# One VectorE add moved ahead of two others in the first pair of six passes

## The chip, the cores and the metric

The kernel runs on one core of one Trainium2 chip. The time is the device time of one execution in microseconds (us); a smaller number is better. Every run named here is with a granted TensorE clock of 0.999 to 1.0.

## The reference

```python
h = x @ w1                         # x: 8 x 1024 x 1024, w1: 1024 x 4096
h = 0.5 * h * (1 + np.tanh(np.sqrt(2 / np.pi) * (h + 0.044715 * h ** 3)))
return (h @ w2).astype(np.float32) # w2: 4096 x 1024
```

Two matrix products with a gelu between them, for 8192 rows.

## The kernel before

The rows are worked in eight blocks of 1024. Each block has a pass called m1 (x @ w1 and the gelu) and a pass called m2 (times w2). Both use a scheme of seven products in place of eight block products; from the third block on (`sb > 1`), products 2 and 3 of m1 are once more split in this way, into seven parts each. An m1 goes through 16 column chunks in eight pairs `j`, with `h` the half of a pair. PSUM banks collect the products, ScalarE (ACT) copies a bank into a float32 buffer, and VectorE (DVE) adds later sums to it. `steps(m, ...)` is a generator that issues one split product in three stages:

```python
part(1, chain, True)                     # PE, into the left half of bank z
part(2, banks[0][:, left], fresh)
yield add(acc[0][:, left], chain)        # DVE reads the chain     (t0L for product 3)
part(6, chain)                           # PE writes the chain again
part(3, banks[0][:, right])
yield add(acc[0][:, right], chain)       # (t0R for product 3)
part(7, chain)
part(5, c5, fresh)
part(4, banks[1][:, left])
add(acc[1][:, left], chain)
... # two more adds for product 2, three for product 3
```

The body of a pair, with cuts:

```python
two = steps(2, source, cs, banks_b, a)
for h in range(2):
    ...                                  # in a first pair: a stage of two, five(h)
for _ in two:
    pass
for h in range(2):
    add(a[h], banks_b[h])                # DVE, 512 columns each
difference(j - 1)
...
def six(h):
    product(banks_a[h], source, 6, cs[h], False)
    act_copy(t[h], banks_a[h])
three = steps(3, source, cs, banks_c, t)
...                                      # not the last pair:
    first = j == 0
    five(0)
    if not first:
        gelu("11", cs[0], a[0])
    five(1)
    six(0)
    if not first:
        gelu("11", cs[1], a[1])
    if 3 in inner:
        next(three)                      # parts 1 and 2, t0L
        six(1)
        for h in range(2 if first else 0):
            gelu("11", cs[h], a[h])
        next(three)                      # parts 6 and 3, t0R
        seven(0)
        next(three)                      # part 7 and the rest
        seven(1)
```

In a first pair (`j == 0`) product 5 is already done inside product 2, so nothing but the adds stands between product 2 and `six(0)`. The helper `tt` in line 119 issues every add of VectorE; line 438 issues every matmul of m1, line 902 those of most m2 passes.

Of the kernel before, what the change touches and what calls it, by code (L numbers as in the profile page):

```python
# [61 lines left out]
def kernel(  # L62
# [46 lines left out]
    def psum():  # L109
        return pp.tile([P, HT], F32, name="ps")  # L110
# [23 lines left out]
    def act_copy(out, in_):  # L134
        tc.keep_in_program_order(nc.scalar.copy(out=out, in_=in_))  # L135
# [296 lines left out]
    def matmul1(xs, sb, quads, start=None):  # L432
        g = {b: gp.tile([P, NI, HT], GT, name=f"g{b}") for b in ("11", "12", "21", "22")}
        inner = INNER_1 if sb > 1 else ()
        left, right = slice(0, HT // 2), slice(HT // 2, HT)

        def multiply(bank, w, x, k, n, first):
            tc.keep_in_program_order(nc.tensor.matmul(  # L438
                bank, lhsT=w, rhs=x, start=first and k == 0, stop=k == n - 1, skip_group_check=not first,
            ))  # L440

        def product(bank, source, m, c, first):
            ops = source.chunk(m, c)
            for k in range(KH):
                multiply(bank, ops[:, k, :], xs[m][:, k, :], k, KH, first)

        def add(out, in1, in0=None):
            tt(out, out if in0 is None else in0, in1, ADD, True)
# [5 lines left out]
        def steps(m, source, cs, banks, acc):  # L454


            fresh = m == 2
            if m not in inner:
                yield product(banks[0], source, m, cs[0], fresh)
                yield  # L460
                yield product(banks[1], source, m, cs[1], fresh)
                return
            z = psum()
            c5 = banks[1][:, right] if fresh else z[:, right]
            chain = z[:, left]

            def part(j, out, first=False):
                for k in range(2):
                    if j in S_TERM:
                        h, b = (int(d) - 1 for d in S_TERM[j])  # L470
                        w = source.ops[m][:, 2 * b + k, h * P:(h + 1) * P]
                    else:
                        w = source.sums[m][:, list(S_SUM).index(j), k, :]
                    if j in W_TERM:
                        b, t = (int(d) - 1 for d in W_TERM[j])
                        x = xs[m][:, 2 * b + k, t * HT // 2:(t + 1) * HT // 2]
                    else:
                        x = xs.inner[m][:, SUMS.index(j), k, :]
                    multiply(out, w, x, k, 2, first)

            part(1, chain, True)
            part(2, banks[0][:, left], fresh)
            yield add(acc[0][:, left], chain)
            part(6, chain)
            part(3, banks[0][:, right])
            yield add(acc[0][:, right], chain)
# [4 lines that stand above are left out]
            add(acc[1][:, right], chain)  # L491
            add(acc[0][:, right], c5)
            if not fresh:
                add(acc[1][:, right], c5)
            yield
# [46 lines left out]
        for j in range(NI // 2):  # L542
            cs = (2 * j, 2 * j + 1)
            end = j == NI // 2 - 1
            if sb > 1:
                quads += [StoredHalf(i) for i in range(len(quads), min(j + 3, NI // 2))]
                source = quads[j]
            else:
                source = quads[j // 2]
            if start is not None and j == 0:  # L550
                start.pair(gelu)
                ahead(j)
                continue
            jobs = list(ahead(j))
            banks_a = [psum(), psum()]
            a = [temp(), temp()]
            for h in range(2):
                product(banks_a[h], source, 1, cs[h], True)
                act_copy(a[h], banks_a[h])
            banks_c, p5, t = [], [], [temp(), temp()]  # L560

            def five(h):
                if len(p5) == h:
                    banks_c.append(psum())
                    p5.append(temp())
                    product(banks_c[h], source, 5, cs[h], True)
                    act_copy(p5[h], banks_c[h])

            banks_b = [psum(), psum()]
            two = steps(2, source, cs, banks_b, a)  # L570
            more = xs.inner_jobs(3) if j == 0 and sb > 1 and 3 not in xs.inner else []
            for h in range(2):
                if late is not None:
                    gelu("12", late[1][h], late[3][h])
                if j == 0 or 2 in inner:
                    next(two)
                if late is not None:
                    product(late[2][h], late[0], 4, late[1][h], False)
                    gelu("21", late[1][h], late[2][h])
                elif j == 0:  # L580
                    for job in more[2 * h:2 * h + 2]:
                        job()
                    five(h)
            for _ in two:
                pass
            for h in range(2):
                add(a[h], banks_b[h])
            difference(j - 1)
            half = (len(jobs) + 1) // 2
            if start is not None and j == 1:  # L590
                rest = jobs[2:]
                half, jobs = 2, [lambda m=m: quads[0].sum(m, (2, 2), True) for m in (7, 4)] + jobs[:2]
            elif start is not None and j == 2:
                half, jobs = 2, rest
            if sb == 1:
                half = 3 if j % 2 else 0
                if j != 4:
                    jobs += splits
                    splits = []
            for job in jobs[:half]:  # L600
                job()
            def six(h):
                product(banks_a[h], source, 6, cs[h], False)
                act_copy(t[h], banks_a[h])

            def seven(h):
                product(banks_a[h], source, 7, cs[h], False)
                add(p5[h], banks_a[h])

            three = steps(3, source, cs, banks_c, t)  # L610
            if end:
                six(0)
                gelu("11", cs[0], a[0])
# [3 lines that stand above are left out]
                    five(h)  # L617
                for h in range(2):
                    seven(h)
                    gelu("22", cs[h], p5[h])  # L620
                    next(three)
                for h in range(2):
                    product(banks_a[h], source, 4, cs[h], False)
                    gelu("21", cs[h], banks_a[h])
                    for _ in three:
                        pass
                for h in range(2):
                    add(t[h], banks_c[h])
                    gelu("12", cs[h], t[h])
            else:  # L630
# [6 lines that stand above are left out]
                if not first:  # L637
                    gelu("11", cs[1], a[1])
                if 3 in inner:
                    next(three)  # L640
                    six(1)
                    for h in range(2 if first else 0):
                        gelu("11", cs[h], a[h])
                    next(three)
                    seven(0)
                    next(three)
                    seven(1)
                else:
# [3 lines that stand above are left out]
                    for _ in three:  # L652
# [3 lines that stand above are left out]
                for _ in three:  # L656
                    pass
                for h in range(2):
                    gelu("22", cs[h], p5[h])
                for h in range(2):  # L660
                    add(t[h], banks_c[h])
                late = (source, cs, banks_a, t)
            for job in jobs[half:]:
                job()
            if sb == 1 and j < 2 * len(SPLIT_IN_M1):
                splits = split_in_m1(SPLIT_IN_M1[j // 2], j % 2)
            steady(j)
# [361 lines left out]
    first = First()  # L1029
# [39 lines left out]
```

## Time and profile before

| | before |
|---|---|
| time, first three runs | 1487.91 us (1487.71 to 1488.25) |
| span of the profiled run | 1486.0 us |
| PE busy | 99% |
| VectorE busy | 77% |
| PE's waits for VectorE's adds, as shown | 2.3 us, 7 stops |

PE is the bound. What it loses to other engines is small, and of what the views show nearly all sits in six places. The prediction shows the lines. Two things help to read them. A group or a timeline row with a count merges several instructions. And the end of a matmul in the trace is modelled (one of 512 columns is shown 0.379 us long where starts are 0.216 us apart, one of 256 columns 0.272 us where they are 0.109 us apart), so the idle time shown before a matmul can be shorter than the delay of its start. I therefore count a **loss** from start to start: the distance of two matmuls' starts less the usual distance, 0.216 us after 512 columns and 0.109 us after 256. Counted like this, the six places lost 3.09 us; the six passes also have one stop of 0.325 us at 637 us, and 41 of 0.043 to 0.047 us, 1.9 us together, that no view lists.

### The profile page before, as it was taken

To read this page: it belongs to the slowest core of one execution; us is meant where nothing else is said; L and a number is where in the kernel's file an instruction comes from. 1 tells how busy PE (TensorE), PEld (TensorE's weight loads), DVE (VectorE), ACT (ScalarE), POOL (GpSimd) and SP (SyncE) were. 2 spreads that over 40 slices of the span, in tenths; PEclk is the share of its full clock that TensorE was granted. 3 is DMA by queue.
4 is the path that set the end of the run, shared out by engine and by line. 5 is a ranking of instruction groups with operands and counts; after the bars stand their busy time and mean duration, and the time that the engine had idled before them with its cause. 6 is when DMAs were issued, how large, how long until landed. Compare 5 with 4: busy or idle time off the path is not lost.

```text
span 1486.0 us, 26324 instructions
## 1 busy us (share of the span) xinstructions
PE 1477.3 (99%) x9879; PEld 964.2 (65%) x9879; DVE 1149.5 (77%) x1792; ACT 613.3 (41%) x1154; POOL 231.8 (16%) x311
## 2 busy tenths in 40 slices
PE   9999999999999999999999999999999999999998
PEld 5444444444455787558875588655886568855687
DVE  6657458767677898779987799877997779877887
ACT  5665026621166412663136621366214652056510
POOL 2542222222211012100022001210111101101011
PEclk9999999999999999999999999999999999999999
DMA  9999798987997999989999899998999989997886
GB/s 331 340 355 404 202 363 291 405 269 228 383 288 173 358 306 308 336 203 386 303 307 340 222 364 307 311 305 244 353 305 321 307 263 340 294 373 240 297 279 212
DMA packets 242719, 453.70 MB, mean 305 GB/s; under 512 B 80672, under 2 KB 85792, under 8 KB 241696
## 3 DMA queue, kind: packets, MB, share of 16 engines
q1 hardware_dynamic: 215680, 358.69, 71.6%
q0 software_dynamic: 26912, 93.34, 21.3%
q8 instruction: 77, 1.26, 0.3%
q14 instruction: 50, 0.41, 0.1%
HBM read 355.47 MB, written 111.15 MB: 314 GB/s over the span
## 4 chain that ended last, share of the span: by engine, by line
PE 97%; DVE 1%; DMA 1%; issue 0%; ACT 0%; DVEq 0%
PE ps L438 49%; PE ps L902 35%; PE ps L943 13%; PE ps L368 1%; DVE tmp L119 1%; DMA out_dram<-tmp 0%; PE ps L345 0%; DMA u<-in_x_dram 0%; DVE u L119 0%; ACT u L135 0%; ACT tmp L135 0%; PE ps L303 0%; DVE tmp L337 0%; DVE u L356 0%; DVEq L119 0%
## 5 line engine op out<-in xcount | busy, mean ns | idle before, releaser
L438 PE MATMUL ps<-u 128*128 128x512 f16 (+1 forms) x4104 | 746.7, 344 | 2.3 <-DVE tmp L119 2.3
L119 DVE TENSOR_TENSOR tmp<-tmp,ps 128x256 f32<-128x256 f32 (+1 forms) x930 | 450.7, 532 | 273.9 <-PE ps L438 169.4
L438 PEld LDWEIGHTS <-u 128*128 128x128 f16 x4104 | 401.1, 98 | 345.3 <-issue 11.0
L135 ACT COPY tmp<-ps 128x512 f32<-128x512 f32 x410 | 231.3, 581 | 302.1 <-PE ps L438 154.1
L451 ACT ACTIVATE g<-tmp 128x512 f16<-128x512 f32 x378 | 238.1, 633 | 165.2 <-DVE tmp L119 165.0
L902 PE MATMUL ps<-u,gc 128*128 128x256 f16 x2688 | 300.4, 273 | 0.0
L902 PEld LDWEIGHTS <-gc 128*128 128x128 f16 x2688 | 262.5, 98 | 31.2
L902 PE MATMUL ps<-u,g 128*128 128x256 f16 x2016 | 227.9, 273 | 0.0
L119 DVE TENSOR_TENSOR u<-u 128x2048 f16<-128x2048 f16 (+3 forms) x292 | 219.5, 790 | 9.2 <-DMA raw_d<-u 2.5
L135 ACT COPY u<-ps 128x512 f32<-128x512 f32 (+1 forms) x134 | 77.9, 587 | 348.9 <-PE ps L902 341.4
L902 PEld LDWEIGHTS <-g 128*128 128x128 f16 x2016 | 197.3, 98 | 24.1
L689 POOL DMA_DIRECT2D out_dram<-u x70 | 64.0, 989 | 710.5 <-issue 366.0
L119 DVE TENSOR_TENSOR u<-u,ps 128x512 f32<-128x512 f32 x216 | 147.7, 684 | 34.7 <-PE ps L902 28.5
L943 PE MATMUL ps<-u,g 128*128 128x512 f16 x768 | 166.4, 379 | 0.0
L943 PEld LDWEIGHTS <-g 128*128 128x128 f16 x768 | 75.1, 98 | 90.6
L119 DVE TENSOR_TENSOR g<-g,g 128x2048 f16<-128x2048 f16 (+1 forms) x136 | 130.3, 980 | 1.6 <-ACT g L451 1.6
L119 DVE TENSOR_TENSOR gc<-g,gc 128x2048 f16<-128x2048 f16 x84 | 102.4, 1219 | 0.6
L119 DVE TENSOR_TENSOR gc<-g 128x2048 f16<-128x2048 f16 x78 | 95.0, 1218 | 0.0
L451 ACT ACTIVATE g<-ps 128x512 f16<-128x512 f32 x134 | 79.9, 597 | 13.9 <-PE ps L438 6.9
L138 POOL CAST u<-gc 128x1024 f16<-128x1024 f32 x40 | 47.2, 1190 | 64.7 <-DMA gc<-in_w_dram 61.7
L415 POOL COPY pace<-g 128x2 f16<-128x2 f16 x24 | 4.4, 185 | 191.4 <-ACT g L451 191.4
L536 POOL TENSOR_TENSOR gc<-g 128x2048 f16<-128x2048 f16 x6 | 24.4, 4063 | 62.1 <-ACT g L451 62.1
(37 smaller groups left out, 257.3 us busy)
## 6 DMA issues: line engine op xcount, KB each, us to landing
u<-w_d SPq DMA_DIRECT2D x336, 256.0 KB, 6.5
u<-in_d SPq DMA_DIRECT2D x168, 512.0 KB, 7.1
u<-raw_d SPq DMA_DIRECT2D x252, 256.0 KB, 7.1
out_dram<-u POOLq DMA_DIRECT2D x70, 512.0 KB, 9.3
gc<-in_w_dram SPq DMA_DIRECT2D x48, 512.0 KB, 6.3
u<-in_d SPq DMA_DIRECT2D x96, 256.0 KB, 7.4
raw_d<-u SPq DMA_DIRECT2D x32, 512.0 KB, 8.9
u<-raw_d SPq DMA_DIRECT2D x32, 512.0 KB, 14.1
```

Of the source, the lines that this page charges most:

```text
L119: i = nc.vector.tensor_tensor(out=out, in0=in0, in1=in1, op=op)
L135: tc.keep_in_program_order(nc.scalar.copy(out=out, in_=in_))
L138: pool_last[0] = nc.gpsimd.tensor_copy(out=out, in_=in_)
L368: tc.keep_in_program_order(nc.tensor.matmul(bank[:, cols], lhsT=w[:, k, :], rhs=self.xs.blocks[f"{a}{r}"][:, k, cols], start=r == 1 and k ...
L415: mark = nc.gpsimd.tensor_copy(out=pace, in_=g_chunk[:, :2])
L438: tc.keep_in_program_order(nc.tensor.matmul(bank, lhsT=w, rhs=x, start=first and k == 0, stop=k == n - 1, skip_group_check=not first,))
L451: gelu_last[0] = nc.scalar.activation(out=g[b][:, c, :], in_=src, func=GELU)
L536: nc.gpsimd.tensor_tensor(out=early[7], in0=u, in1=v, op=SUB)
L689: return nc.gpsimd.dma_start(out=rows, in_=src, **kw)
L902: tc.keep_in_program_order(nc.tensor.matmul(bank[:, i * OH // 2:(i + 1) * OH // 2], lhsT=t[:, c, i * P:(i + 1) * P], rhs=self.y[j][:, c, : ...
L943: tc.keep_in_program_order(nc.tensor.matmul(pair(bank), lhsT=a[:, c, :], rhs=chunks(pieces[c // QC])[:, :, c % QC, :], start=(first and c ...
```

## The change

The intent: in the first pair of each of the six later m1 passes, let the first chain sum of product 3 (t0L) run before the two sums that end product 2, so that PE need not wait for it.

```diff
@@ -566,8 +566,21 @@
+            sixes = []
+
+            def six(h):
+                if h not in sixes:
+                    sixes.append(h)
+                    product(banks_a[h], source, 6, cs[h], False)
+                    act_copy(t[h], banks_a[h])
...          # seven and three are defined here too
             for _ in two:
                 pass
+            if j == 0 and 3 in inner:
+                six(0)
+                next(three)
             for h in range(2):
                 add(a[h], banks_b[h])
             difference(j - 1)
...
                 if 3 in inner:
-                    next(three)
+                    if not first:
+                        next(three)
                     six(1)
```

More of the change, by code (lines that the diff above doesn't have):

```diff
@@ L567, in five, with seven @@
                     act_copy(p5[h], banks_c[h])
+            sixes = []
[4 more added lines that the diff above has]
+                    act_copy(t[h], banks_a[h])
+            def seven(h):
+                product(banks_a[h], source, 7, cs[h], False)
+                add(p5[h], banks_a[h])
             banks_b = [psum(), psum()]
             two = steps(2, source, cs, banks_b, a)
+            three = steps(3, source, cs, banks_c, t)
             more = xs.inner_jobs(3) if j == 0 and sb > 1 and 3 not in xs.inner else []
@@ L601, in matmul1 @@
                 job()
-            def six(h):
-                product(banks_a[h], source, 6, cs[h], False)
-                act_copy(t[h], banks_a[h])
-            def seven(h):
-                product(banks_a[h], source, 7, cs[h], False)
-                add(p5[h], banks_a[h])
-            three = steps(3, source, cs, banks_c, t)
             if end:
```

## The prediction

The 1.73 us: from durations and pitches of the trace of the kernel before. In that trace an add of a bank took 0.67 to 0.69 us for 512 columns and 0.41 to 0.42 us for 256. That VectorE takes its adds in the order of its queue is read from the same trace: t0L's input was ready at 768.99 us, but t0L started at 769.49, behind the two sums. So is part 6's wait for t0L: t0L ended at 769.908 and part 6 started at 769.962. The eight banks that one rival counts are the pool of the program (`bufs=8`).

> **What bounds the kernel now.** I read the page first, then the PE's waits, then the chain of waits, then the timeline of one first pair instruction by instruction. The page's first part and its groups (engine, op, tiles, shape, count | busy us, mean ns | idle before, releaser):
>
> ```profile
> PE 1477.3 (99%) x9879; PEld 964.2 (65%) x9879; DVE 1149.5 (77%) x1792; ACT 613.3 (41%) x1154; POOL 231.8 (16%) x311
> ...
> L438 PE MATMUL ps<-u 128*128 128x512 f16 (+1 forms) x4104 | 746.7, 344 | 2.3 <-DVE tmp L119 2.3
> ```
>
> PE is busy for 1477.3 of 1486.0 us at full clock, so this change, which removes no matmul, can only win idle PE time. All idle time of the multiplication line that has a releaser is 2.3 us, and the releaser is the add helper of VectorE. The waits of PE give the same as a count:
>
> ```profile
> PE ps L438 <- DVE tmp L119: 2.3, 7, 0.6
> PE ps L303 <- DVE warm L1027: 1.2, 1, 1.2
> ```
>
> Seven waits. The whole chain of waits, in order of time, places them: it leaves PE for a run of VectorE adds ending at 409.5, 589.7, 769.9, 949.8, 1129.7 and 1309.7 us, which are the first pairs (j = 0) of the six later m1 passes, and once at 637.0, in a later pair. The piece of it for one first pair (start, us, what):
>
> ```profile
> 762.52 4.56 PE ps L438 x26
> ...
> 767.17 0.10 DVE tmp L119
> 767.27 0.24 issue
> 767.51 0.76 DVE tmp L119 x2
> 768.29 0.35 DVE tmp L119
> 768.65 0.25 issue
> 768.90 1.02 DVE tmp L119 x2
> 769.96 86.83 PE ps L438 x502
> ```
>
> After it PE runs 86.83 us without a break, so a microsecond won here comes off the end. Now the timeline of that pair, engine by engine. In program order VectorE ends product 2 with three 256-column adds of the chain and of the fifth term, then adds banks_b[0] and banks_b[1] (512 columns each), then the first chain sum of product 3, here called t0L:
>
> ```profile
> 767.17 1.08 DVE L119 TENSOR_TENSOR tmp<-tmp,ps 128x256 f32<-128x256 f32 x3 [0.28 <-PE ps L438]
> 768.29 1.28 DVE L119 TENSOR_TENSOR tmp<-tmp,ps 128x512 f32<-128x512 f32 x2
> 769.49 0.41 DVE L119 TENSOR_TENSOR tmp<-tmp,ps 128x256 f32<-128x256 f32 x1
> 770.38 0.42 DVE L119 TENSOR_TENSOR tmp<-tmp,ps 128x256 f32<-128x256 f32 x1 [0.47 <-PE ps L438]
> ```
>
> The third line is t0L, the fourth the second chain sum of product 3 (t0R). ScalarE copies product 6 (first line: t[0]), which t0L needs, and PE's part 6 of product 3 must wait until t0L has read the chain's bank:
>
> ```profile
> 768.40 0.59 ACT L135 COPY tmp<-ps 128x512 f32<-128x512 f32 x1 [0.93 <-PE ps L438]
> 769.70 0.59 ACT L135 COPY tmp<-ps 128x512 f32<-128x512 f32 x1 [0.71 <-PE ps L438]
> ```
>
> ```profile
> 769.96 0.60 PE L438 MATMUL ps<-u 128*128 128x256 f16 x4 [0.30 <-DVE tmp L119]
> ```
>
> t0L's input was ready at 768.99 (the copy's end), but it started at 769.49 because the two 512-column adds stood ahead of it. That is the fault that the change goes after.
>
> The shown 0.30 us of idle time is too small. Single matmuls of 512 columns start 0.216 us apart but are shown as 0.379 us long; so 0.163 us of every stop after one is hidden under its modelled end. From start to start, PE lost 0.459 us here: the last product-6 matmul started at 769.287, the next was due at 769.503 and came at 769.962. Counted like this over the trace, the six first pairs lost 0.446, 0.809, 0.459, 0.459, 0.456 and 0.460 us, together **3.09 us**. The 0.809 is the pair at 589.8: there VectorE's first add of the run began 0.35 us later after PE than in the others, for a reason that the trace does not give.
>
> [...]
>
> **The change part by part.** It adds and removes no instruction. For ScalarE and PE the order stays the same too: in a first pair product 5 has already been done inside product 2, so product 6 of half 0 was already PE's next work. What moves is one VectorE instruction: t0L goes ahead of the adds of banks_b[0] and banks_b[1]. It happens once in each of six m1 passes (inner product 3 exists only there).
>
> I work it out from s, the start of the last matmul of product 6, half 0 (767.987 in the pair above), with durations and pitches of that pair.
> 1. PE would be ready for part 6 at 0.216 + 4 x 0.109 (parts 1 and 2) + 4 x 0.216 (product 6, half 1) = s + 1.516.
> 2. The copy of t[0] starts at s + 0.416 and takes 0.586. An add that waits for ScalarE starts 0.033 later (the steady pairs: copies that end 33 ns before t0L starts), so t0L starts at s + 1.035; VectorE has been free since s + 0.27. t0L takes 0.42, and PE follows an add's end by 0.054: s + 1.51. So the wait at part 6 disappears. The steady pairs, which have this order already, lose 0.046 us there, with a busier ScalarE.
> 3. Part 6 and part 3 (4 x 0.109) and product 7, half 0 (4 x 0.216) follow; PE is then due for part 7, on the same chain, at s + 1.516 + 0.436 + 0.864 = s + 2.816. Part 7 must wait for t0R to read the chain.
> 4. VectorE's queue is now t0L, banks_b[0], banks_b[1], t0R. Start-to-start times: 0.338 after a 256-column add out of idle, 0.605 between 512-column adds, 0.597 from one of them to the next: t0R starts at s + 1.035 + 0.338 + 0.605 + 0.597 = s + 2.575, ends 0.414 later, and part 7 can start at s + 3.043.
> 5. So a **new wait of 0.227 us** stands at part 7, where there was none: before, t0R came right after part 6 and ended 0.46 us ahead of part 7's start (770.80 against 771.26).
> 6. After that VectorE is no worse off than before: the add of product 7 starts about s + 2.91 where it started at s + 3.47, and the rest follows PE.
>
> Net per pair: 0.446 - 0.227 = 0.22, four times about 0.458 - 0.227 = 0.23 (0.93 together), and 0.809 - 0.227 = 0.58 in the pair with the late add (its t0L waits for a copy ending at 588.46, and VectorE is free at 588.08, so the lateness is absorbed). Sum 0.22 + 0.93 + 0.58 = **1.73 us**. The loss of 3.09 us falls to 1.36 us. 1487.91 - 1.73 = 1486.2 us, 0.12% less.
>
> The two gelus of block 11 need the adds that now come later: banks_b[1] is summed at s + 1.978 + 0.68 = s + 2.66, and its gelu started at s + 2.73 before (770.715). It moves by little, and ScalarE is at 41%.
>
> **The rivals.** *All of it comes back* (1484.8 us): part 7 would not wait. For it: the change was presumably meant so. Against it: t0R stands behind two adds of 0.6 us each, and the sum of step 4 has only measured pitches in it. Part 7's dependence on t0R is in the code (same chain tile), hidden today by 0.46 us of slack.
>
> *The wait only moves* (1487.9 to 1489 us): t0L, now at the head of a FIFO and waiting for ScalarE, leaves VectorE idle from about s + 0.27 to s + 1.035, some 0.76 us that it used for the two sums. If a further hold of a few tenths comes in behind t0L, like the unexplained 0.35 us at 587, the new wait equals the old one. For it: the new wait is already half the old. Against it: VectorE has no other work queued in this stretch.
>
> *Another bank* (1489 to 1492 us): product 3's chain bank is now requested before the sums of product 2 are issued. If it got a bank that waits for one of them, PE would stop at part 1. Against it: of eight banks six are in use, product 2's chain is done and one is free; before, part 1 started (768.20) ahead of the sum of banks_b[0] (768.29), so it did not use that bank.
>
> **Range and chances.** The middle case takes 1.73 us, the full one 3.1, the moved one 0 or less. The three runs before span 1487.71 to 1488.25, a spread of 0.5 us. That gives 1485.3 to 1487.5 us. A change of 2% would be 30 us; only some 3.1 us of waits are touched, so nearly all the chance is on "same".
>
> **What would show it.** Right: in each first pair t0L starts some 0.46 us earlier after product 6, the wait before part 6 is gone, and a stop of about 0.23 us, shown as only 0.06 idle, stands before the first matmul of part 7; the PE's waits for VectorE fall from 2.3 to about 0.5 us shown; the span falls by about 1.7 us; the number of matmuls stays. The prediction is wrong if part 7 doesn't wait (then near 1484.8), if part 6 still waits, or if PE stops at part 1 of product 3 or at the first product of the next pair.

## The result, and the profile after

The changed kernel takes 1486.09 us (median of six, 1485.82 to 1486.73) against 1488.15 us (six runs, 1487.71 to 1488.64) of the kernel before. The ratio is 0.9987, with a 95% interval of 0.9974 to 1.0. Ratios here are the mean time of one kernel's fast runs over that of the other's of the same rounds, so not quite the ratio of the medians. A second set of five runs gave 1486.13 us and 0.9986 (0.9973 to 0.9998). Measured against 2% it is the same; the 1486.2 us foretold is 0.1 us off.

The page after, the line of engines and the group of m1's matmuls:

```profile
PE 1476.1 (99%) x9879; PEld 962.5 (65%) x9879; DVE 1146.3 (77%) x1792; ACT 613.5 (41%) x1154; POOL 225.3 (15%) x311
...
L438 PE MATMUL ps<-u 128*128 128x512 f16 (+1 forms) x4104 | 746.6, 344 | 0.5 <-DMA u<-w_d 0.2
```

The number of matmuls is unchanged, and the idle time in front of them fell from 2.3 to 0.5 us. PE's waits after (engine and line, what it waited for: us in total, times, longest):

```profile
PE ps L345 <- DVE tmp L337: 2.2, 4, 0.9
PE ps L303 <- DVE warm L1035: 1.2, 1, 1.2
PE ps L368 <- ACT u L135: 0.5, 1, 0.5
PE ps L368 <- DVE u L196: 0.4, 1, 0.4
PE ps L438 <- DMA u<-w_d: 0.2, 1, 0.2
```

The row in which line 438 waits for line 119 is gone; the 0.2 us for a transfer is the stop at 637 us, which was there before, under another releaser. Taken alone this view would say that all is won.

The spans of the two profiled runs, 1486.0 and 1485.0 us, differ by only 1.0 us. The start explains most of that: the first m1 matmul came at 27.15 us before and at 27.82 us after. It is not the change's doing. In the traces of the experiments below it came at 27.74 us in e1, which has the order of the kernel before, and at 27.16 us in e4, which has the order of the change.

The chain of waits after, for the pair that the prediction worked through (start, us, what):

```profile
762.28 5.86 PE ps L438 x34
768.13 0.02 issue
768.16 0.59 ACT tmp L135
768.75 0.03 issue
768.78 1.96 DVE tmp L119 x4
770.74 0.04 issue
770.78 85.54 PE ps L438 x494
```

The chain still leaves PE, now for the copy of product 6 and then for four adds. The timeline of VectorE shows these four: t0L, the two sums, t0R.

```profile
768.78 0.42 DVE L119 TENSOR_TENSOR tmp<-tmp,ps 128x256 f32<-128x256 f32 x1 [0.76 <-ACT tmp L135]
769.12 1.28 DVE L119 TENSOR_TENSOR tmp<-tmp,ps 128x512 f32<-128x512 f32 x2
770.31 0.41 DVE L119 TENSOR_TENSOR tmp<-tmp,ps 128x256 f32<-128x256 f32 x1
```

And PE's timeline has the matmul that waited for the last of them, the first of part 7, with no idle time printed in brackets at all:

```profile
770.78 0.81 PE L438 MATMUL ps<-u 128*128 128x256 f16 x6
```

It is a stop all the same. The matmul before it started at 770.342 and this one at 770.779, 0.437 us later instead of 0.216: PE lost 0.221 us. The trace holds 0.058 us of idle time here, which is too short for the views.

The stretch from the first m1 matmul to the first m2 matmul of each later block, read from the traces, is free of the start's noise:

| block | before | after | e1 | e2 | e3 | e4 | e6 |
|---|---|---|---|---|---|---|---|
| third | 94.26 | 94.04 | 94.26 | 94.17 | 93.82 | 94.63 | 93.82 |
| fourth | 94.90 | 94.32 | 94.90 | 94.44 | 94.32 | 94.92 | 94.03 |
| fifth | 94.28 | 94.04 | 94.27 | 94.17 | 93.82 | 94.63 | 93.82 |
| sixth | 94.29 | 94.07 | 94.28 | 94.18 | 93.84 | 94.64 | 93.82 |
| seventh | 94.27 | 94.04 | 94.27 | 94.17 | 93.82 | 94.64 | 93.82 |
| eighth | 94.28 | 94.04 | 94.27 | 94.17 | 93.82 | 94.63 | 93.82 |
| sum | 566.28 | 564.54 | 566.26 | 565.30 | 563.44 | 568.09 | 563.15 |

The sums are of the unrounded stretches. Before less after is 1.75 us. The six m1 stretches hold what the change won; the columns e1 to e6 belong to the experiments. Of the runs without a column, r_after sums to 564.50, e5 to 563.15 and e7 to 563.09 us.

### The profile page after: what moved, and what is told of

It reads as the page before. It is cut to its first block, busy times and chain, and to the rows that moved or that the text cites. A ratio compares the mean times of both kernels' runs of the same rounds, so it can differ in the third digit from the quotient of the medians.

```text
span 1485.0 us, 26324 instructions
## 1 busy us (share of the span) xinstructions
PE 1476.1 (99%) x9879; PEld 962.5 (65%) x9879; DVE 1146.3 (77%) x1792; ACT 613.5 (41%) x1154; POOL 225.3 (15%) x311
## 4 chain that ended last, share of the span: by engine, by line
PE 96%; DMA 2%; DVE 1%; ACT 0%; SPq 0%; issue 0%; DVEq 0%
PE ps L438 48%; PE ps L910 35%; PE ps L951 13%; PE ps L368 1%; DVE tmp L119 1%; DMA gc<-in_w_dram 1%; DMA u<-in_d 1%; DMA u<-w_d 1%; DMA u<-raw_d 0%; ACT tmp L135 0%; SPq L132 0%; PE ps L345 0%; DVE u L196 0%; DVE u L119 0%; DVE u L356 0%
```

## The experiments

The **theory**: the order of VectorE's queue alone decides. t0L early frees part 6; the two sums, now between t0L and t0R, hold part 7. **Rivals**: the early product 6 (or its copy) is what helps; part 7's stop belongs to a bank or to product 7 and not to the queue; VectorE has slack there.

All kernels gave correct results. The first four shared their rounds and the runs of the kernel before (1487.83 us, nine runs), and so did the last four (1488.33 us, nine runs), on another chip. So e3 and the runs built on it were never timed side by side: their difference is read from the traces. An edit is shown against the changed kernel unless another is named.

**e1_six_only: product 6 early, product 3 not.**

```diff
             if j == 0 and 3 in inner:
                 six(0)
-                next(three)
...
                 if 3 in inner:
-                    if not first:
-                        next(three)
+                    next(three)
```

> Only product 6 is moved ahead in the program text; the first part of product 3 and its chain sum t0L stay behind the two sums. No engine's own order differs from the kernel before. Queue theory (what counts is t0L's place in VectorE's queue): the same time as before, 1488.1 us within 0.5, and the six first pairs again lose 0.45 to 0.46 us before part 6 (0.8 in the pair of the fourth m1), 3.09 us together. Rival (the early product 6 or its copy is what helps): near the changed kernel, 1486.1 us.

Measured: 1487.9 us (1487.51 to 1488.65), ratio 1.0 (0.9987 to 1.0012). Its waits of PE:

```profile
PE ps L438 <- DVE tmp L119: 2.3, 7, 0.6
```

That is the line of the kernel before, and the losses are 0.443, 0.806, 0.458, 0.454, 0.459 and 0.456 us. So writing product 6 earlier in the program does nothing, and what worked is t0L's place in the queue. It is a check of the method too: a rewritten program with the old order on each engine has the old losses to within 0.005 us.

**e2_sums_last: the two sums behind t0R.**

```diff
             if j == 0 and 3 in inner:
                 six(0)
                 next(three)
-            for h in range(2):
-                add(a[h], banks_b[h])
+            else:
+                for h in range(2):
+                    add(a[h], banks_b[h])
...
                     six(1)
+                    next(three)
                     for h in range(2 if first else 0):
+                        add(a[h], banks_b[h])
                         gelu("11", cs[h], a[h])
-                    next(three)
                     seven(0)
```

> From the changed kernel, the two 512-column sums go behind t0R (and the two gelus with them). Queue theory: part 7 no longer waits, because t0R now starts when part 6 is done, about s + 1.93, and ends near s + 2.35 while part 7 is due at s + 2.816; all 3.09 us of the first pairs come back: 1485.0 us (1484.6 to 1485.4), no stop over 0.05 us left in a first pair. Rival (part 7 waits for something else, such as product 7 or a bank): the stop of 0.22 us stays and the time is 1486.1 us. Third possibility: the sums now land on the adds of product 7 and the chain sums after part 7, and a stop appears later, at the first product of the next pair.

Measured: 1487.37 us (1486.66 to 1487.9), ratio 0.9995 (0.9982 to 1.0007). My number was missed by more than 2 us. The stop before part 7 did go, as the theory wants. In its place PE lost 0.351 to 0.354 us in each of the six passes some 5 us later. VectorE's and PE's timelines, and the chain, of the same block:

```profile
769.27 5.73 DVE L119 TENSOR_TENSOR tmp<-tmp,ps 128x256 f32<-128x256 f32 x12 [0.48 <-PE ps L438]
```

```profile
775.05 1.24 PE L438 MATMUL ps<-u 128*128 128x256 f16 x7 [0.19 <-DVE tmp L119]
```

```profile
769.27 4.57 DVE tmp L119 x10
773.85 0.08 issue
773.93 1.08 DVE tmp L119 x2
775.01 0.04 issue
775.05 80.99 PE ps L438 x468
```

From t0R on, twelve adds follow one another without a gap for 5.73 us. The last is the first chain sum of product 2 in the second pair, and part 6 of that product waits for it. The third possibility of the expectation came true, though at this add and not at the pair's first product. An idle stretch of VectorE ahead of t0L had been given away, and the debt of two sums ran on through the queue to the next place where PE depends on it.

**e3_one_each: one sum ahead of t0L, one behind.**

```diff
-            if j == 0 and 3 in inner:
-                six(0)
-                next(three)
             for h in range(2):
                 add(a[h], banks_b[h])
+                if h == 0 and j == 0 and 3 in inner:
+                    six(0)
+                    next(three)
```

> Queue order banks_b[0], t0L, banks_b[1], t0R: one sum in the idle time ahead of t0L, one between. Queue theory with the measured pitches: the sum of banks_b[0] ends near s + 0.99, before t0L's copy is there (t0L at s + 1.035 as in the changed kernel), t0R starts at s + 1.97 and ends at s + 2.39, 0.4 us ahead of part 7: no stop at either place, 1485.0 us (1484.6 to 1485.4). If any sum put between t0L and t0R makes part 7 wait, a stop of 0.1 to 0.2 us would stay and the time be 1485.5 to 1486.1 us.

Measured: 1485.38 us (1484.99 to 1485.62), ratio 0.9981 (0.9968 to 0.9995). The chain of waits over the same block as above:

```profile
762.07 93.82 PE ps L438 x544
```

The chain no longer leaves PE in this pass. In five of the six passes no stop is left in the first pair; in the fourth block PE lost 0.227 us at part 6. There VectorE's run of adds begins 0.35 us late, so the sum of banks_b[0] ends at 588.947 and t0L starts at 588.866 instead of about 588.62. The theory's main claim holds: one 0.6 us sum between t0L and t0R makes nobody wait, two do. By the table e3 takes 1.10 us off the changed kernel's 564.54.

**e4_extra_add: a third add between t0L and t0R.**

```diff
             for h in range(2):
                 add(a[h], banks_b[h])
+            if j == 0 and 3 in inner:
+                tt(extra, extra, extra, ADD, True)   # scratch, set to 0 at the start
```

> The changed kernel with one more 512-column add (on a scratch tile of its own, result unused) between the sums and t0R, once in each of the six first pairs; one memset more at the start. Queue theory: part 7's stop grows from 0.22 by a pitch of 0.60 to 0.82 us in each, 3.6 us in all: 1489.7 us (1489.2 to 1490.2). Rival (VectorE has slack there and the stop has another cause): 1486.1 us. Aside: the late VectorE instruction in the fourth m1 stands at place 831 of the engine's traced instructions before and after; if that goes by place and not by instruction, it is now at place 831 again, two instructions earlier in the program.

Measured: 1490.31 us (1489.37 to 1490.81), ratio 1.0014 (1.0001 to 1.0026). VectorE's timeline, then PE's:

```profile
769.64 1.28 DVE L119 TENSOR_TENSOR tmp<-tmp,ps 128x512 f32<-128x512 f32 x2
770.84 0.68 DVE L119 TENSOR_TENSOR extra<-extra 128x512 f32<-128x512 f32 x1
771.44 0.41 DVE L119 TENSOR_TENSOR tmp<-tmp,ps 128x256 f32<-128x256 f32 x1
```

```profile
771.90 1.46 PE L438 MATMUL ps<-u 128*128 128x256 f16 x9 [0.66 <-DVE tmp L119]
```

The losses are 0.817 to 0.822 us in all six, where 0.82 was expected. The six stretches grow by 568.09 - 564.54 = 3.55 us, 0.59 each: the stop before part 7 follows VectorE's queue one for one. The time lies 0.1 us above the range expected; in this trace the stretch from the last block's first m2 matmul to the end was also 0.83 us longer than in e3's (90.49 against 89.66 us), which the theory doesn't cover. The aside gave a hint: the fourth block's late first add is gone. VectorE's stream was shifted by two instructions there (the memset and the extra add of the third block), and place 831 of the traced stream is now an add of operands that runs behind other work.

**r_after: the changed kernel again.** Its expectation and result:

> The changed kernel once more, for the comparison within these rounds: 1.2 to 2.1 us under the kernel before; six stops of 0.22 us before part 7 in its trace.

Measured: 1486.13 us (1485.83 to 1486.51), ratio 0.9986. Losses before part 7: 0.215 to 0.218 us, six times.

**e5_gelu_later: ScalarE's order in the other pairs.** On top of e3:

```diff
                 five(0)
-                if not first:
-                    gelu("11", cs[0], a[0])
                 five(1)
                 six(0)
-                if not first:
-                    gelu("11", cs[1], a[1])
+                for h in range(0 if first else 2):
+                    gelu("11", cs[h], a[h])
```

> From e3_one_each; in pairs after the first, ScalarE's first gelu of block 11 goes behind the copy of product 6, half 0. Theory: the 0.045 to 0.048 us that PE loses before part 6 in each of 36 later pairs comes from that copy starting late behind the gelu; the copies come on time, the losses go, and 36 times 0.046 is 1.66 us: about 1.5 to 1.7 us under e3_one_each, 1483.3 to 1484.2 us. Rival: the 0.046 us is what the wait itself costs at the shortest, or the copy of half 1, now behind two gelus, stops something later: no gain or a loss. The six losses of 0.04 us in the last pairs stay, as those pairs are not touched.

Measured: 1484.56 us (1484.47 to 1485.73), ratio 0.9977 (0.9965 to 0.999). The expected range is missed, and the theory fell: every one of the 36 losses is still there, at 0.046 to 0.048 us. In the traces e5 is 0.29 us below e3. ScalarE's timeline in a later pair:

```profile
779.93 0.58 ACT L135 COPY tmp<-ps 128x512 f32<-128x512 f32 x1 [0.33 <-PE ps L438]
```

This is product 6's copy. ScalarE is idle for 0.33 us ahead of it, so no gelu is in its way. Yet the copy starts 0.471 us after the last matmul of product 6 started (779.456), and in a first pair 0.416 us. In e3's trace, with the gelu ahead, the same copy also started 0.471 us after that matmul (779.227 to 779.698): the gelu had not been what held it. In the trace the later pair's copy has a separate wait instruction for PE in front (779.871) and itself waits for ScalarE's own semaphore; the first pair's copy has one wait only. The 0.055 us between the two fit the 0.046 us lost. In the whole trace of e5, where an idle ScalarE was released by PE, work behind a separate instruction that waited for PE started 0.078 to 0.079 us after the release in 197 of 201 places, and work that itself waited for PE after 0.023 to 0.024 us everywhere. But no run takes the second wait away, so this cause is read and not shown. What e5 did win sits in the fourth block's fifth pair, where e3 loses 0.325 us and e5 only 0.046 (see e6).

**e6_places: nothing but six small instructions at the start.** On top of e3:

```diff
     nc.scalar.activation(out=warm, in_=warm, func=GELU)
+    shift = consts.tile([P, 1], F32, name="shift")
+    for _ in range(2):
+        tc.keep_in_program_order(nc.vector.memset(shift, 0.0))
+    for _ in range(4):
+        act_copy(shift, warm)
```

> From e3_one_each; two small memsets on VectorE and four one-column copies on ScalarE are put in at the very start, nothing else. Place theory (an engine comes late by about 0.35 us at fixed places in its instruction stream, places 831 on VectorE and 703 on ScalarE, whatever instruction stands there): the late first add in the fourth m1's first pair and the late copy in its fifth pair go, and with them the stops of 0.227 and 0.325 us: 0.55 us less PE loss than e3_one_each. Rival (it belongs to the instruction or to the moment, for example to transfers then in flight): both stops stay as they were.

Measured: 1484.79 us (1484.43 to 1485.38), ratio 0.9977 (0.9963 to 0.9991). The waits of PE, all that the view lists:

```profile
PE ps L303 <- DVE shift L1039: 1.2, 1, 1.2
PE ps L345 <- DVE tmp L337: 0.8, 1, 0.8
PE ps L368 <- ACT u L135: 0.6, 1, 0.6
```

No line of m1 is left. Both stops of the fourth block, 0.227 and 0.325 us, are gone; a loss of 0.091 us at 635.6 and one of 0.166 us at 653.3 came in. ScalarE again shows a delay of 0.336 us at place 703 of its stream, now at an earlier instruction. So it goes by place. Against e3 the six stretches fall by 0.29 us, less than the 0.55 expected, because of the two new losses.

**e7_both: e5 and e6 together.**

> The edits of e5_gelu_later and e6_places together. If both theories hold and add up: 1.66 + 0.55 us under e3_one_each, about 1482.8 to 1483.6 us; as the late gelus change how many waiting instructions ScalarE's stream has, its late place may land elsewhere and leave one stop of about 0.3 us.

Measured: 1484.58 us (1484.4 to 1485.02), ratio 0.9976 (0.9963 to 0.9988). The expected 1482.8 to 1483.6 us was missed. With the gelu theory fallen, e7 could be no more than e6, and it is not: 1484.58, 1484.79 and 1484.56 us (e7, e6, e5) cannot be told apart. One stop of 0.166 us, at 653.5 us, is left in its trace, the one that came in with e6. All three beat the kernel before, and their medians lie 1.3 to 1.6 us below r_after's in the same rounds. The intervals of the ratios overlap, so their lead on the changed kernel rests on the stops that the traces no longer have.

## Why the prediction was right

The step numbers are the prediction's; s was 767.742 us in the pair of the profile after.

- Step 1, part 6 due at s + 1.516: it started at 769.258, s + 1.516. The wait before it is gone.
- Step 2, t0L at s + 1.035: it started at 768.777, s + 1.035.
- Step 4, t0R at s + 2.575: 770.310, s + 2.568.
- Step 5, a new stop of 0.227 us before part 7: 0.221 us here, 0.218 to 0.221 in all six. e3 removed it by taking one sum out from between, and e4 raised it by 0.60 with one more, so its cause is shown.
- Step 6, the add of product 7 at s + 2.91: it came at 770.759, s + 3.02, about 0.1 us later than put, and earlier than before (s + 3.47). Nothing waited for it, so this did not matter.
- The fourth block's lateness was absorbed: its loss fell from 0.809 to 0.219 us. This is why its stretch fell by 0.59 us and the others by 0.22 to 0.24.
- The sum: 1.73 us foretold, 1.75 us in the traces (1.79 in r_after's). The two timed ratios, 0.9987 and 0.9986, put it at 1.9 to 2.1 us, with an interval of some 2 us to each side. So it is the traces that confirm the size. That the time itself agreed to 0.1 us is partly luck: the kernel before came out at 1488.15 us in six runs where the prediction subtracted from 1487.91, and the medians differ by 2.06 us.

Of the rivals, "all of it comes back" is what e3 comes to in five of six passes, by another order. "The wait only moves" happened to e2. "Another bank" did not occur: no stop stands at part 1 in any trace.

One reading of the prediction needs a word. The 86.83 us that PE runs "without a break" after the stop hold seven of the stops of 0.043 to 0.047 us. One reading aid of the prediction was off: it expected about 0.5 us of shown waits for VectorE, and the waits view showed none, because six stops of 0.055 to 0.058 us shown are below what it lists.

## What to carry to other kernels

When an instruction is moved ahead in a queue that is worked in order, as VectorE's was in these traces (t0L, ready at 768.99 us, started at 769.49 behind two sums), work out when the next instruction that another engine waits for will come, and not only the one that was moved: what was overtaken now stands in front of something else. Put the overtaken work into idle time of the queue, as e3 did with one sum on either side (1485.38 us), rather than behind everything, as e2 did (1487.37 us). For stops of a few tenths of a microsecond, count from start to start of the matmuls: six stops of 0.218 to 0.221 us were shown here as 0.055 to 0.058 us of idle time.

## What else the traces showed

- After a 512-column matmul a stop is shown 0.163 us too short (0.379 shown against a pitch of 0.216), so six real stops of 0.22 us vanished from the views.
- VectorE and ScalarE came late at fixed places of their traced streams: 447, 831 and 1471 on VectorE, 703 and 1215 on ScalarE, the same before and after, all leaving 63 when divided by 128. From the wait instruction to the work behind it took 0.415 to 0.436 us there against a usual 0.066 on VectorE, and 0.336 against 0.057 us on ScalarE. e6 shows that place 703 and not the instruction counts (0.336 us again); in the fourth block it cost PE 0.325 us. No run shows the cause.
- Where a separate instruction waited for PE ahead of a copy, the copy started 0.471 us after the last matmul's start instead of 0.416, and work behind such a wait started 0.078 to 0.079 us after PE's release instead of 0.023 to 0.024 (the trace of e5).
- The start of the kernel shifted from trace to trace: the first m1 matmul came anywhere from 27.15 to 27.83 us in these traces, and at 27.15 and 27.74 us in two kernels with the same order on every engine. That is more than a third of the 1.75 us studied. Whether it goes by execution or by program stays open: each program has one trace but the changed kernel, whose two have 27.82 and 27.77 us.
